# A two-layer decoder trunk on one core: the order of loads and weight splits in the wide phases of its MLP

## The chip, the cores and the metric

The kernel runs on one core of a Trainium2 chip. The metric is device time in microseconds of one execution; the number for the kernel before is the median of three runs. A profile of one execution, taken on the chip, gives spans, waits and transfers. In it PE is TensorE's matmuls, PEld its weight loads, DVE is VectorE, ACT is ScalarE, POOL is GpSimd and SP is SyncE. A "q" behind an engine's name (SPq) means its queue of issued transfers.

## The reference

The reference is a decoder trunk of two layers over 256 positions of width 2048, in float32. Each layer is a token mixer and then a gated MLP; each half is wrapped in RMS norms. The mixer of layer 0 is dilated window attention beside cross-attention to 256 memory tokens; that of layer 1 is stick-breaking attention beside the same cross-attention. The change touches the MLP, which is the same in both layers:

```python
def _conv_ffn(h, w_up, w_conv, b_conv, w_down):
    S = h.shape[1]
    u = h @ w_up
    gate, val = jnp.split(u, 2, axis=-1)
    gp = jnp.pad(gate, ((0, 0), (CONV_WIDTH - 1, 0), (0, 0)))
    acc = b_conv + gp[:, CONV_WIDTH - 1:CONV_WIDTH - 1 + S] * w_conv[CONV_WIDTH - 1]
    for j in range(CONV_WIDTH - 1):
        acc = acc + gp[:, j:j + S] * w_conv[j]
    return (jax.nn.silu(acc) * val) @ w_down
```

Here `h` is 256 x 2048, `w_up` is 2048 x 11264 (5632 gate columns, then 5632 value columns), the convolution runs over three positions, and `w_down` is 5632 x 2048.

## The kernel before, in words

**Precision.** Every product of two float32 matrices is made of three matmuls in a faster 32-bit format. Each operand is split into a high part (a rounding cast) and a low part (what the cast lost). `split` (L600) does it: ScalarE casts (L601), VectorE subtracts (L602). `mm3` (L127) then multiplies high by high, low by high and high by low.

**The MLP.** `ffn` (L724) walks over eleven groups of 512 columns of the gate and the value. Six groups are "narrow": they go tile by tile, 128 columns of one weight matrix against all positions. Five, those in `WIDE` (1, 3, 5, 7, 9), are "wide": `wide` (L613) makes the 512 gate and 512 value columns of a group for all 256 positions at once, with seven block products in place of eight, as in Strassen's scheme. It needs sums of weight blocks and sums of activation blocks. The activation sums are made once a layer by `sums_of_h` (L575); its last pieces are put behind the first wide phase's work by `rest` (L887). Behind each wide phase but the last, `downs` (L754) multiplies two finished groups by `w_down`.

**A wide phase** has eight units, u = 0 to 7, one for 256 rows of the weights. A unit holds:
- seven products of three matmuls each, `product` (L634), in seven PSUM banks: products 1, 2 and 3 with plain weights, products 7, 5, 6 and 4 with weight sums;
- one tile of the next narrow group beside them, `ws_beside` (L152). It is a Python generator in five steps: load the tile's weights of 1 MB (L156) and split the first half; split the second half; sixteen pairs of matmuls with the first half (L163); sixteen with the second half; the tile's sum out of PSUM, a copy on ScalarE (L175) and an addition on VectorE (L176). The eighth PSUM bank is the only one for it, so a tile's first matmul waits for the sum L176 of the tile before;
- the next unit's weights: `load` (L637) fetches 768 KB of raw weights (L640), `sums` (L643) makes two sums on VectorE (L646, L647), `plain` (L650) splits one and a half thousand columns of them, and `split_sums` (L659) splits the sums at the start of the next unit;
- for the unit after that, `first_sums` (L605): SyncE loads 512 KB (L608), and GpSimd adds another block to it with an accumulating transfer (L609) once the first has landed;
- two steps of elementwise work that earlier tiles left behind, run by `catch_up` (L91): the convolution, SiLU and the split of an activation pair.

**Buffers.** Raw weights of every kind share three buffers (`raw`); the high and low parts have four buffers each (`whi`, `wlo`); weight sums, activations and attention tensors share eleven (`sh`).

**Order.** A tile framework orders the instructions of each engine and places all waits. An instruction passed through `pin` (L96) is kept behind the one written before it on its engine, while `self.pinned` is set; it is set from the start of the unit loop (L673) to the end of the phase (L720). In the kernel before this holds matmuls, splits, sums and elementwise work of a phase, but not its loads: the framework may issue L156, L608 and L640 on SyncE in another order than the written one. The first load of raw weights (L663) and of the tile's weights (L669) stand ahead of L673. The written order of a unit's middle is:

```python
            if more:
                raw = load(u + 1)
                t = sums(ahead.pop(0), raw)
                after = beside[u + 1]()
                next(after)
            self.catch_up()
            next(b)
            next(b, None)
            if more:
                f = plain(raw)
                next(after)
```

In words: load the next unit's raw weights, sum them, load the next tile's weights and split their first half, do a leftover step, second half of this tile's matmuls, this tile's sum, then the plain splits, and the second half of the next tile's weights. On SyncE a unit writes the weight sum of u + 2 first (L685 or L687), then the raw weights of u + 1, then the tile's weights of u + 1.

Of the kernel before, what the change touches and what calls it, by code (L numbers as in the profile page):

```python
# [45 lines left out]
class Body:  # L46
# [49 lines left out]
    def pin(self, ins):  # L96
        return self.tc.keep_in_program_order(ins) if self.pinned else ins
# [54 lines left out]
    def ws_beside(self, out, src, h, done=None):  # L152


        raw = self.sb.tile([P, 2048], F32, name="raw", tag="raw", bufs=3)
        self.nc.sync.dma_start(raw, src)  # L156
        parts = []
        for i in range(2):
            parts.append([self.sb.tile([P, 1024], F32R, name=k, tag=k, bufs=4) for k in ("whi", "wlo")])
            self.split(*parts[i], raw[:, i * 1024:(i + 1) * 1024])  # L160
            yield
        b = self.bank("s")
        mm = lambda *o, **k: self.pin(self.nc.tensor.matmul(*o, **k))  # L163
        for half, (whi, wlo) in enumerate(parts):
            for k in range(8):
                kt = half * 8 + k
                ks = slice(k * P, (k + 1) * P)
                both, one = h[2][:, kt, :, :].rearrange("p a t -> p (a t)"), h[0][:, kt, :]
                if kt < KT - 1:
                    mm(b, whi[:, ks], both, start=kt == 0, stop=False)  # L170
                mm(b[:, 0:S], wlo[:, ks], one, start=False, stop=False)
                if kt == KT - 1:
                    mm(b, whi[:, ks], both, start=False, stop=True)
            yield
        self.pin(self.nc.scalar.copy(out, b[:, S:]))  # L175
        self.pin(self.nc.vector.tensor_add(out, b[:, 0:S], out))  # L176
        if done:
            done()
# [426 lines left out]
    def first_sums(self, src, u):  # L605

        d = self.sh([P, 1024])
        self.nc.sync.dma_start(d, src[u][:, 512:1536])  # L608
        self.nc.gpsimd.dma_start(d.rearrange("p (a n) -> p a n", a=2),  # L609
                                 src[u][:, 1536:].unsqueeze(1).to_broadcast([P, 2, 512]), accum_op=ALU.add)  # L610
        return d

    def wide(self, src, then, ahead, h, s, forms, r, beside):  # L613

        nc, n = self.nc, KT // 2
        ps = {i: self.bank("g" if i in (1, 2, 6, 7) else "s") for i in range(1, 8)}
        pin, add = self.pin, nc.vector.tensor_add
        half = lambda f, i: f[..., i * 512:(i + 1) * 512]

        def lhs(i, u):
            if i in (1, 2, 4):
                kt, t = 2 * u + (i != 1), int(i == 4)  # L630
                return [h[2][:, kt, a, t * P:(t + 1) * P] for a in range(2)]
            return [s[:, u, {5: 0, 6: 1, 7: 2, 3: 3}[i], a, :] for a in range(2)]

        def product(i, u, f, at):  # L634
            self.mm3(ps[i], *lhs(i, u), half(f[0], at), half(f[1], at), u == 0, u == n - 1)

        def load(u):  # L637

            raw = self.sb.tile([P, 2048], F32, name="raw", tag="raw", bufs=3)
            nc.sync.dma_start(raw[:, :1536], src[u][:, :1536])  # L640
            return raw

        def sums(d, raw):  # L643

            e = self.sh([P, 1024])
            pin(add(half(e, 1), half(d, 0), half(raw, 2)))  # L646
            pin(add(half(e, 0), half(e, 1), half(raw, 0)))  # L647
            return d, e

        def plain(raw):  # L650
            fa, fb = ([self.sb.tile([P, 1024], F32R, name=k, tag=k, bufs=4) for k in ("whi", "wlo")]
                      for _ in range(2))
            self.split(*fa, raw[:, 0:1024])
            self.split(*(half(f, 0) for f in fb), half(raw, 2))
            return fa, fb

        summed = [[forms[:, 2 * i + j, :] for j in range(2)] for i in range(2)]

        def split_sums(t):  # L659
            for of, parts in zip(t, summed):  # L660
                self.split(*parts, of)

        raw = load(0)  # L663

        high, low = self.splits[-4]
        with self.tc.issue_after(high.ins), self.tc.issue_after(low.ins):
            t = sums(ahead.pop(0), raw)
            split_sums(t)
        b = beside[0]()  # L669
# [3 lines that stand above are left out]
        self.pinned = True  # L673
        for u in range(n):
            more = u + 1 < n
            next(b)
            if u:
                split_sums(t)
            self.catch_up()
            fa, fb = f  # L680
            product(1, u, fa, 1)
            product(2, u, fa, 0)
            product(3, u, fb, 0)
            if u + 2 < n:
                ahead.append(self.first_sums(src, u + 2))  # L685
            elif then is not None:
                ahead.append(self.first_sums(then, u + 2 - n))  # L687
            if more:
                raw = load(u + 1)
                t = sums(ahead.pop(0), raw)  # L690
                after = beside[u + 1]()
                next(after)
            self.catch_up()
            next(b)
            next(b, None)
            if more:
                f = plain(raw)
                next(after)
            product(7, u, summed[0], 1)
            product(5, u, summed[0], 0)  # L700
            product(6, u, summed[1], 1)
            product(4, u, summed[1], 0)
            b = after
        a, g0, v0, v1 = (self.sc([P, 512]) for _ in range(4))
        more = lambda out, x, i: pin(add(out, ps[i], x))

        def scaled(out, i, t):
            pin(nc.vector.scalar_tensor_tensor(out, ps[i], r[:, t:t + 1], out, op0=ALU.mult, op1=ALU.add))

        pin(nc.scalar.copy(a, ps[1]))  # L710
        pin(nc.scalar.activation(g0, ps[1], AF.Copy, scale=r[:, 0:1]))  # L711
        scaled(g0, 2, 0)
        more(a, a, 6)
        more(v0, a, 5)
        more(v0, v0, 3)
        more(a, a, 7)
        more(v1, a, 5)
        pin(nc.scalar.activation(a, a, AF.Copy, scale=r[:, 1:2]))
        scaled(a, 4, 1)
        self.pinned = False  # L720
        self.catch_up(-1)
        return (g0, a), (v0, v1)
# [480 lines left out]
```

## Time and profile before

| what | value |
|---|---|
| three runs | 2288.51, 2296.90 and 2276.14 us; median 2288.51 |
| the profiled execution's own time | 2280.21 us |
| its span in the trace | 2278.4 us |
| TensorE matmuls busy | 2206.8 us (97%) |
| VectorE busy | 1651.4 us (72%) |
| ScalarE busy | 1283.7 us (56%) |
| TensorE clock granted, mean | 0.991 |
| transfers, mean rate | 227 GB/s |
| the ten wide phases, from first matmul to last product | 910.93 us |

The profile is of one execution. Matmuls overlap, so a busy TensorE is not TensorE at its peak. "Idle before <- X" gives the time an engine did nothing in front of an instruction, and what ended that; where an instruction waits for several things, the one that came last is named. The stretches view gives, for a window of time, the busy time of each engine, the number of its instructions, the granted clock and the share of time in which the sixteen DMA engines moved data. Line numbers in the profile are those of the kernel file.

### The profile page before, as it was taken

To read this page: it belongs to the slowest core of one execution; us is meant where nothing else is said; L and a number is where in the kernel's file an instruction comes from. 1 tells how busy PE (TensorE), PEld (TensorE's weight loads), DVE (VectorE), ACT (ScalarE), POOL (GpSimd) and SP (SyncE) were. 2 spreads that over 40 slices of the span, in tenths; PEclk is the share of its full clock that TensorE was granted. 3 is DMA by queue.
4 is the path that set the end of the run, shared out by engine and by line. 5 is a ranking of instruction groups with operands and counts; after the bars stand their busy time and mean duration, and the time that the engine had idled before them with its cause. 6 is when DMAs were issued, how large, how long until landed. Compare 5 with 4: busy or idle time off the path is not lost.

```text
span 2278.4 us, 28873 instructions
## 1 busy us (share of the span) xinstructions
PE 2206.8 (97%) x10962; PEld 1845.7 (81%) x10962; DVE 1651.4 (72%) x2175; ACT 1283.7 (56%) x1844; POOL 148.6 (7%) x168
## 2 busy tenths in 40 slices
PE   9999999989999999999999999999899999999998
PEld 7888888868878788787888888877688787887886
DVE  6567767977876867777774677579777768677786
ACT  7556556555555565555664555465565555656563
POOL 0000000010101111010000000000101011110100
PEclk9999999999999999999999999999999999999999
DMA  8745457676978979787745445576768789787974
GB/s 323 265 170 188 166 183 249 205 221 211 275 226 257 277 218 271 221 256 252 277 166 185 159 159 174 193 240 203 219 225 265 220 255 275 217 263 241 269 253 182
DMA packets 102381, 516.78 MB, mean 227 GB/s; under 512 B 10465, under 2 KB 10849, under 8 KB 61921
## 3 DMA queue, kind: packets, MB, share of 16 engines
q1 hardware_dynamic: 72288, 439.43, 54.5%
q0 software_dynamic: 29952, 75.51, 16.4%
q8 instruction: 86, 1.41, 0.2%
q14 instruction: 55, 0.44, 0.1%
HBM read 491.82 MB, written 23.07 MB: 226 GB/s over the span
## 4 chain that ended last, share of the span: by engine, by line
PE 78%; DMA 11%; DVE 5%; ACT 2%; issue 2%; SPq 0%; POOL 0%; POOLq 0%; ACTq 0%; DVEq 0%
PE ps_g L128 36%; PE ps_s L163 13%; PE ps_g L145 12%; PE ps_g L146 7%; DMA sh<-in_uw_dram 6%; PE ps_s L128 6%; DMA raw<-in_up_dram 4%; DVE wlo L602 3%; ACT whi L601 2%; PE ps_g L148 1%; PE ps_s L877 1%; DMA raw<-in_dn_dram 1%; PE ps_s L279 1%; DVE qk L176 0%; DMA raw<-in_wmv_dram 0%
## 5 line engine op out<-in xcount | busy, mean ns | idle before, releaser
L602 DVE TENSOR_TENSOR wlo<-raw,whi 128x1024 fp32r<-128x1024 f32 (+1 forms) x758 | 867.2, 1162 | 412.6 <-ACT whi L601 401.2
L601 ACT CAST whi<-raw 128x1024 fp32r<-128x1024 f32 (+1 forms) x758 | 743.8, 1003 | 665.8 <-DMA raw<-in_up_dram 273.2
L163 PE MATMUL ps_s<-h,whi 128*128 128x512 f32 x1280 | 477.0, 408 | 48.5 <-DVE qk L176 48.5
L128 PE MATMUL ps_g<-whi,sh 128*128 128x512 f32 x1488 | 466.1, 394 | 7.9 <-ACT sc L711 6.5
L145 PE MATMUL ps_g<-h,whi 128*128 128x512 f32 x1200 | 430.3, 401 | 0.8 <-DVE h L269 0.8
L163 PE MATMUL ps_s<-h,wlo 128*128 128x256 f32 x1280 | 352.7, 286 | 0.0
L146 PE MATMUL ps_g<-h,wlo 128*128 128x256 f32 x1280 | 345.8, 280 | 0.0
L163 PEld LDWEIGHTS ps_s<-h,whi 128*128 128x128 f32 x1280 | 247.1, 193 | 115.5 <-DVE qk L176 59.8
L128 PEld LDWEIGHTS ps_g<-whi,sh 128*128 128x128 f32 x1488 | 276.6, 188 | 71.4 <-ACT sc L711 10.9
L128 PE MATMUL ps_g<-wlo,sh 128*128 128x512 f32 x744 | 292.0, 393 | 0.0
L128 PE MATMUL ps_g<-whi,h 128*128 128x512 f32 x880 | 274.8, 393 | 0.5 <-ACT whi L601 0.5
L145 PEld LDWEIGHTS ps_g<-h,whi 128*128 128x128 f32 x1200 | 225.4, 188 | 52.1 <-DVE h L269 1.1
L163 PEld LDWEIGHTS ps_s<-h,wlo 128*128 128x128 f32 x1280 | 248.4, 194 | 9.6
L146 PEld LDWEIGHTS ps_g<-h,wlo 128*128 128x128 f32 x1280 | 241.6, 189 | 6.3
L602 DVE TENSOR_TENSOR x<-sh,x 128x1024 fp32r<-128x1024 f32 x160 | 189.1, 1217 | 0.0
L128 PEld LDWEIGHTS ps_g<-whi,h 128*128 128x128 f32 x880 | 160.0, 189 | 34.0 <-ACT whi L601 0.9
L128 PE MATMUL ps_g<-wlo,h 128*128 128x512 f32 x440 | 172.6, 393 | 1.1 <-DVE wlo L602 1.0
L601 ACT CAST x<-sh 128x1024 fp32r<-128x1024 f32 x160 | 161.4, 1049 | 9.0 <-DMA sh<-in_uw_dram 6.9
L128 PEld LDWEIGHTS ps_g<-wlo,sh 128*128 128x128 f32 x744 | 139.7, 188 | 31.8
L609 POOL DMA_DIRECT2D sh<-in_uw_dram x80 | 95.7, 1196 | 754.3 <-DMA sh<-in_uw_dram 497.3
L128 PE MATMUL ps_g<-x,h 128*128 128x512 f32 x480 | 137.6, 394 | 0.0
L128 PE MATMUL ps_s<-x,h 128*128 128x512 f32 x480 | 137.3, 394 | 0.0
(180 smaller groups left out, 2025.7 us busy)
## 6 DMA issues: line engine op xcount, KB each, us to landing
raw<-in_up_dram SPq DMA_DIRECT2D x96, 1024.0 KB, 5.4
raw<-in_dn_dram SPq DMA_DIRECT2D x88, 1024.0 KB, 6.4
raw<-in_uw_dram SPq DMA_DIRECT2D x80, 768.0 KB, 7.4
sh<-in_uw_dram SPq DMA_DIRECT2D x80, 512.0 KB, 9.0
sh<-in_uw_dram POOLq DMA_DIRECT2D x80, 512.0 KB, 10.0
raw<-in_wqk_a_dram SPq DMA_DIRECT2D x24, 1024.0 KB, 4.8
yout<-sh POOLq DMA_DIRECT2D x32, 512.0 KB, 8.3
raw<-in_wo_b_dram SPq DMA_DIRECT2D x16, 1024.0 KB, 4.9
```

Source lines behind the costliest of these rows:

```text
L128: mm = lambda *o, **k: self.pin(self.nc.tensor.matmul(*o, **k))
L145: mm(b, whi[:, ks], both, start=kt == 0, stop=False)
L146: mm(b[:, 0:S], wlo[:, ks], one, start=False, stop=False)
L148: mm(b, whi[:, ks], both, start=False, stop=True)
L163: mm = lambda *o, **k: self.pin(self.nc.tensor.matmul(*o, **k))
L279: self.nc.tensor.transpose(b[:, k * S + t * P:k * S + (t + 1) * P], self.x[:, t, kt * P:(kt + 1) * P], self.ident)
L601: high = self.pin(self.nc.scalar.copy(hi, of))
L602: low = self.pin(self.nc.vector.tensor_sub(lo, of, hi.bitcast(F32)))
L609: self.nc.gpsimd.dma_start(d.rearrange("p (a n) -> p a n", a=2), src[u][:, 1536:].unsqueeze(1).to_broadcast([P, 2, 512]), accum_op=ALU.add)
L877: nc.tensor.transpose(b[:, j * S + t * P:j * S + (t + 1) * P], of[t][:, f:f + P], self.ident)
```

## The change

It has two parts. The three kinds of loads in a wide phase are passed through `pin`, so that SyncE issues them in the written order: weight sum, raw weights, tile's weights. And in the middle of a unit the plain splits move from behind the tile's sum to ahead of it, while both halves of the next tile's load and split come behind it, where only the second half was.

```diff
@@ ws_beside @@
         raw = self.sb.tile([P, 2048], F32, name="raw", tag="raw", bufs=3)
-        self.nc.sync.dma_start(raw, src)
+        self.pin(self.nc.sync.dma_start(raw, src))
@@ first_sums @@
         d = self.sh([P, 1024])
-        self.nc.sync.dma_start(d, src[u][:, 512:1536])
+        self.pin(self.nc.sync.dma_start(d, src[u][:, 512:1536]))
@@ wide, load @@
-            nc.sync.dma_start(raw[:, :1536], src[u][:, :1536])
+            pin(nc.sync.dma_start(raw[:, :1536], src[u][:, :1536]))
@@ wide, the unit loop @@
             if more:
                 raw = load(u + 1)
-                t = sums(ahead.pop(0), raw)
                 after = beside[u + 1]()
-                next(after)
+                t, f = sums(ahead.pop(0), raw), plain(raw)
             self.catch_up()
             next(b)
             next(b, None)
             if more:
-                f = plain(raw)
+                next(after)
                 next(after)
```

GpSimd's accumulating transfer (L609) is not held to an order. The number of instructions, transfers and buffers is the same.

## The prediction

> **What bounds the kernel now.** I read the page first, then the stretches (busy time by window) over the wide phases, then the timeline engine by engine around the stalls, then the totals of waits. The page says that TensorE is the bound on average:
>
> ```profile
> span 2278.4 us, 28873 instructions
> PE 2206.8 (97%) x10962; PEld 1845.7 (81%) x10962; DVE 1651.4 (72%) x2175; ACT 1283.7 (56%) x1844; POOL 148.6 (7%) x168
> ...
> PE 78%; DMA 11%; DVE 5%; ACT 2%; issue 2%; SPq 0%; POOL 0%; POOLq 0%; ACTq 0%; DVEq 0%
> ```
>
> The 11% DMA in the chain that ended last says that transfers still end some of TensorE's waits. All that the change edits is in the ten wide phases (five in each layer, eight units each). I cut each phase at the first matmul of its unit 0, at that of unit 6, and behind unit 7's last product. Units 0 to 5, with the sum row over all ten phases last (columns: length; PE, PEld, DVE, ACT, POOL busy; TensorE clock, DMA share, GB/s):
>
> ```profile
> 421.69:494.43 72.74, 65.79 (x319) 53.90 (x318) 58.90 (x82) 36.74 (x50) 4.73 (x4) 0.98 0.74 229
> 570.34:633.34 63.00, 63.00 (x320) 52.98 (x319) 50.79 (x61) 35.65 (x47) 6.77 (x7) 1.00 0.90 280
> 707.48:770.98 63.50, 63.23 (x319) 52.97 (x318) 50.87 (x61) 35.64 (x47) 7.29 (x7) 1.00 0.95 285
> 1559.60:1633.13 73.53, 66.10 (x320) 53.77 (x318) 59.48 (x83) 36.87 (x50) 4.79 (x5) 0.98 0.75 229
> sum 657.02, PE 637.36 PEld 531.47 DVE 525.37 ACT 358.28 POOL 66.78; mean PE 63.74 PEld 53.15 DVE 52.54 ACT 35.83 POOL 6.68
> ```
>
> Units 6 and 7:
>
> ```profile
> 633.34:659.63 26.29, 22.80 (x107) 18.63 (x105) 17.55 (x21) 12.92 (x17) 3.31 (x3) 0.94 0.88 248
> 904.24:932.53 28.29, 23.67 (x107) 19.43 (x105) 19.15 (x23) 14.65 (x20) 3.58 (x3) 0.88 0.87 252
> 2178.36:2199.38 21.02, 21.02 (x107) 17.42 (x105) 17.78 (x22) 13.66 (x19) 0.15 (x1) 1.00 0.70 230
> sum 253.91, PE 224.04 PEld 183.90 DVE 183.44 ACT 140.32 POOL 27.73; mean PE 22.40 PEld 18.39 DVE 18.34 ACT 14.03 POOL 2.77
> ```
>
> The row 570.34:633.34 is six units in 63.00 us with TensorE busy for all 63.00: a unit without a stall takes 10.50 us. Two units take 21.02 in the last row. So the floor is 84 us a phase. Units 0 to 5 of all phases are 657.02 - 630.0 = **27.0 us** over it, of which the first phases of the two layers hold 9.7 + 10.5; units 6 and 7 are 253.91 - 210.0 = **43.9 us** over it. Together 70.9 us: that is all that the change can win. It is idle time and slower matmuls behind it (busy 224.04 against 210, clock 0.88).
>
> **Why units 6 and 7 stall.** The second phase of layer 0, in time (unit 6 begins at 633.34, as the row of units 6 and 7 has it, unit 5 10.5 us before that, unit 4 21):
>
> ```profile
> 613.26 0.33 SPq L156 DMA_DIRECT2D raw<-in_up_dram  x1
> 614.40 0.33 SPq L640 DMA_DIRECT2D raw<-in_uw_dram  x1
> 623.46 0.33 SPq L156 DMA_DIRECT2D raw<-in_up_dram  x1
> 624.60 0.33 SPq L640 DMA_DIRECT2D raw<-in_uw_dram  x1
> 624.98 0.91 SPq L608 DMA_DIRECT2D sh<-in_uw_dram  x2
> ...
> 633.10 2.44 POOL L609 DMA_DIRECT2D sh<-in_uw_dram  x2 [17.67 <-DMA sh<-in_uw_dram]
> ...
> 644.55 0.69 DVE L646 TENSOR_TENSOR sh<-sh,raw 128x512 f32<-128x512 f32 x1 [6.61 <-DMA sh<-in_uw_dram]
> ...
> 647.02 0.42 DVE L176 TENSOR_TENSOR qk<-ps_s,qk 128x256 f32<-128x256 f32 x1
> ...
> 647.49 0.51 PE L163 MATMUL ps_s<-h,whi 128*128 128x512 f32 x1 [3.49 <-DVE qk L176]
> ```
>
> SyncE issues no weight sum between 613 and 624.98, then two at once: unit 7's stands behind two loads that the code writes after it. It lands 8 us later, GpSimd's accumulating transfer (633.10) needs 11.4 more, VectorE waits 6.61 us for it, the tile's sum L176 stands behind that in VectorE's queue, and the next tile's matmul, which needs the same PSUM bank, waits 3.49 us.
>
> **Why the first phases stall in every unit.** Layer 1's first phase, units 2 to 3:
>
> ```profile
> 1585.86 0.33 SPq L156 DMA_DIRECT2D raw<-in_up_dram  x1
> 1598.37 0.33 SPq L156 DMA_DIRECT2D raw<-in_up_dram  x1
> ...
> 1593.24 1.05 ACT L601 CAST whi<-raw 128x1024 fp32r<-128x1024 f32 x1 [6.24 <-DMA raw<-in_up_dram]
> ...
> 1594.32 1.23 DVE L602 TENSOR_TENSOR wlo<-raw,whi 128x1024 fp32r<-128x1024 f32 x1 [3.15 <-ACT whi L601]
> 1595.57 0.42 DVE L176 TENSOR_TENSOR qk<-ps_s,qk 128x256 f32<-128x256 f32 x1
> 1596.52 2.96 DVE L602 TENSOR_TENSOR wlo<-raw,whi 128x1024 fp32r<-128x1024 f32 x3 [0.52 <-ACT whi L601]
> ```
>
> It is a loop. The up load goes out when the plain split frees a `raw` buffer (1585.86), lands 7.4 us later, is split first (ScalarE 1593.24, VectorE 1594.32), then comes the tile's sum (1595.57), then the plain splits (from 1596.52), and these free the buffer for the next up load (1598.37): 12.51 us round, two above the matmuls. Over the kernel:
>
> ```profile
> ACT whi L601 <- DMA raw<-in_up_dram: 273.2, 65, 7.2
> PE ps_s L163 <- DVE qk L176: 48.5, 24, 5.2
> ```
>
> **The change, part by part.** No instruction and no byte is added or taken away.
>
> *Order of loads.* Three loads of a unit are held to the written order on SyncE: weight sum of u+2, raw weights of u+1, up weights of u+1. Behind the up load at 613.26 would come unit 7's sum, not at 624.98: some 10 us earlier. With its own 8.1 + 11.4 us (624.98 to 633.10, 633.10 to 644.55) it would be there at about 634, and unit 6 asks for it at 637.9 (644.55 less the wait of 6.61). The stall of units 6 and 7 goes: -43.9 us. What is queued behind the sum is now the raw load and then the up load; both wait for it if no `sh` buffer is free. I count one `sh` tile for the memory keys (layer 0), four for the activations and four to five for sums at once, of eleven, so I put this wait at nothing; if the cover is missing, both loads and the up tile behind them are late by as much (third rival).
>
> *Plain splits ahead of the tile's sum.* The raw weights are loaded a unit ahead (the load at 614.40, in unit 4, is for the sums that unit 5 makes), so these splits wait for no fresh transfer, and they free `raw` some 3 us (one 1.23 split, L176's 0.42, and the gap in front) earlier. The up load goes out that much sooner and is asked for later, behind the tile's sum: it gets some 11 us to land (a unit of 10.5 us, and a cast's worth more), where it had the 7.4 of the loop. The loop of 12.51 us opens, and with it most of the 27.0 us.
>
> *The next tile's weights split behind the sum.* This is the price. The first split was done before the matmuls ended; now it stands between the tile's sum and the next tile's first matmul. A unit in which TensorE sets the pace has the pieces, since there the same engines do a split of the same size just behind the sum:
>
> ```profile
> 620.25 0.37 ACT L175 COPY qk<-ps_s 128x256 f32<-128x256 f32 x1 [0.33 <-PE ps_s L163]
> 620.52 2.52 ACT L601 CAST whi<-raw 128x1024 fp32r<-128x1024 f32 x3
> ...
> 621.61 2.96 DVE L602 TENSOR_TENSOR wlo<-raw,whi 128x1024 fp32r<-128x1024 f32 x3 [0.53 <-ACT whi L601]
> ...
> 622.84 0.39 PE L163 MATMUL ps_s<-h,whi 128*128 128x512 f32 x1
> ```
>
> Cast 620.52 + 1.05 = 621.57, subtraction 621.61 + 1.23 = 622.84, and the next tile begins at 622.84. It fits with nothing to spare: the low part is due at the second matmul (0.23 us on), its weights must be loaded before that, so I take 0.05 us a unit, 70 units: +3.5 us. From below the price is 0 (the row above); from above it is 0.7 us a unit (the rival of the split). I choose the low end because nothing stands between L175 and the cast in that row.
>
> *VectorE's time.* 50.79 / 6 = 8.5 us a unit of 10.5 (row 570.34), so it holds the pace. In the two first phases it does 58.90 - 50.79 = 8.1 us more (the sums of the activations, in units 0 and 1), 12.5 a unit there: some 5 us of delay stay in each, +10.
>
> *DMA.* In the row 707.48:770.98 the sixteen engines are busy 0.95 of the time at 285 GB/s. Moving a 512 KB sum and its accumulation into units 0 to 5 pushes that to about 1. From below this costs nothing, since 63.50 us were kept at that share; from above the rival below. I take 1.3 us in each of the seven phases in question (not the first ones and not the last, which loads no sums for a successor): +9.
>
> A phase of shorter units asks more of memory, so one more row bears on it, two stretches at the start of layer 0's fourth phase:
>
> ```profile
> 840.00:850.00 10.00, 10.00 (x53) 8.47 (x52) 6.12 (x8) 4.77 (x8) 2.05 (x2) 1.00 1.03 288
> 850.00:860.00 10.00, 10.00 (x53) 8.44 (x52) 6.41 (x7) 3.70 (x5) 1.20 (x1) 1.00 1.07 339
> ```
>
> The Trainium skill, Perfetto Trace Analysis, section Identifying the Most-Contended Engine, says to judge DMA by memory bandwidth used and not by the busy share of its sixteen engines. By that rule 285 of the 339 GB/s seen here leaves room, the +9 falls away and the time would be 2231; the row's share of 0.95 speaks the other way; which of them the kernel follows no row of before can show, and I keep +9.
>
> **Sum.** -70.9 + 3.5 + 10 + 9 = -48.4 us against the profiled execution: 2280.2 (span 2278.4 and 1.8 around it) becomes 2231.8. The runs shown have their median at 2288.5, 8.3 above that execution, so the forecast is **2240 us**, its own range 2222 to 2262.
>
> **Rivals.**
>
> *The DMA engines become the bound.* If the phases hold their pace only up to the 0.90 of the row 570.34:633.34, six units with the 60.3 us of transfers of the row 707.48:770.98 (0.95 of 63.50) need 67.0 us, 4.0 above 63; that is 5.3 for eight units and 37 for seven phases, where the sum has 9: about 2268. For it: the share. Against: that row itself, 63.50 us at 0.95.
>
> *The split behind the sum takes the place of the stall* (the other side). Place: VectorE's and ScalarE's queues between L175 and the next tile. Any lateness of the tile's sum is now followed by 1.05 + 1.23 us in series before TensorE may go on, with only the 2.6 us of four products (620.25 to 622.84) as cover. If the sum comes 1 us late in each of 70 units, because convolution steps, two weight sums and two plain splits all stand ahead of it, that is +70 - 48.4: about 2310. From 0.7 us a unit on it is slower than before. For it: zero slack in the row. Against: 8.5 of 10.5 us of VectorE's work.
>
> *The order does not bring the sums forward.* If the sum of unit 7 still waits for an `sh` buffer until unit 5, units 6 and 7 keep their 43.9 us, and the gain is 27.0 less 13.5: about 2275. For it: SyncE issued no sum in unit 4 (613.26 to 623.46), and a shortage of buffers would do that. Against: the count above.
>
> **How the numbers follow.** Forecast 0.62, DMA bound 0.13, order without effect 0.13, split in the way 0.12. Range 2222 to 2283: it leaves out the last rival and the tail under 2222 (all stalls gone and DMA free would be near 2220). About 1% (23 us, so 2266 and 2311) is what a measurement of this kernel can tell from no change. Faster: 0.62 and part of two rivals, 0.70; same 0.20; slower 0.10.
>
> **What would show it.** Right: a sum issued in every unit and ahead of the raw load; GpSimd's accumulations one per unit; units 6 and 7 near 21 us in the stretches with a clock of 1.00; the waits for up loads far under 273 us. Price right: waits of L163 of under 0.1 us, now ended by L602. Wrong: waits of 1 us ended by L602 in most units (split in the way), VectorE still waiting for `sh<-in_uw` in unit 6 (order), or DMA shares of 1.0 with units of 11 us and more.

## The result and the profile after

The changed kernel takes **2205.45 us** (median of four runs, 2204.71 to 2208.49) beside 2286.61 us for the kernel before in the same comparison (2276.14 to 2296.90). The ratio is 0.965, 95% interval 0.960 to 0.969: 3.5% faster. The forecast of 2240 us had the direction and the two stalls right, but the gain is 35 us larger, and the time lies under the range's low end of 2222.

The page of the changed kernel: its span, the busy times, and the engines' shares of the chain that ended last.

```profile
span 2203.1 us, 28992 instructions
...
PE 2184.6 (99%) x10962; PEld 1837.5 (83%) x10962; DVE 1651.4 (75%) x2175; ACT 1296.0 (59%) x1844; POOL 149.1 (7%) x168
...
PE 96%; DVE 2%; issue 1%; DMA 0%; SPq 0%; ACT 0%; POOL 0%; POOLq 0%; DVEq 0%; ACTq 0%
```

The page counts 119 instructions more than before, none of them among the counted work of the five engines. DMA's 11% of the chain are gone; TensorE's own work makes up 96% of it. The profiled execution took 2204.87 us, 75.3 less than the one of before. The ten wide phases, each now cut as a whole (length; PE, PEld, DVE, ACT, POOL busy; TensorE clock, DMA share, GB/s):

```profile
421.53:508.91 87.38, 85.05 (x425) 70.48 (x424) 78.86 (x107) 53.48 (x70) 8.31 (x7) 1.00 0.91 268
...
684.44:768.51 84.07, 84.07 (x425) 70.72 (x424) 70.64 (x85) 51.82 (x67) 9.25 (x8) 1.00 0.97 289
...
1518.54:1607.14 88.60, 86.34 (x425) 71.85 (x424) 79.04 (x107) 53.39 (x70) 8.34 (x7) 0.98 0.90 265
...
1782.67:1866.74 84.07, 84.07 (x425) 70.72 (x424) 70.54 (x85) 51.91 (x67) 9.23 (x8) 1.00 0.98 291
...
sum 848.55, PE 843.96 PEld 708.12 DVE 722.51 ACT 521.85 POOL 85.19; mean PE 84.40 PEld 70.81 DVE 72.25 ACT 52.18 POOL 8.52
```

The eight later phases sit on the floor of 84 us, with TensorE busy all the time. Only the layers' first phases are longer, by 3.4 and 4.6 us. The phases gave back 910.93 - 848.55 = 62.4 us. That leaves 12.9 us of the span's 75.3 which came from outside the phases. Most of that lies in the eight stretches between two phases of a layer (last row of the view for before, then for after):

```profile
sum 375.90, PE 369.43 PEld 302.46 DVE 258.92 ACT 226.99 POOL 19.09; mean PE 46.18 PEld 37.81 DVE 32.36 ACT 28.37 POOL 2.39
```

```profile
sum 365.83, PE 365.83 PEld 301.76 DVE 247.61 ACT 218.16 POOL 28.84; mean PE 45.73 PEld 37.72 DVE 30.95 ACT 27.27 POOL 3.60
```

That is 10.1 us, and the stretch behind the last phase gave 2.2 more (79.0 to 76.8). In the changed kernel TensorE is busy in every microsecond of these stretches. The prediction did not look at them.

The order of loads in the second phase of layer 0 (unit 4 begins at 596.7, unit 6 at 617.7), SyncE's queue:

```profile
594.83 0.64 SPq L608 DMA_DIRECT2D sh<-in_uw_dram  x1
597.81 0.33 SPq L640 DMA_DIRECT2D raw<-in_uw_dram  x1
603.76 0.33 SPq L156 DMA_DIRECT2D raw<-in_up_dram  x1
604.14 0.42 SPq L608 DMA_DIRECT2D sh<-in_uw_dram  x1
608.32 0.33 SPq L640 DMA_DIRECT2D raw<-in_uw_dram  x1
614.26 0.33 SPq L156 DMA_DIRECT2D raw<-in_up_dram  x1
```

For every unit a sum goes out, ahead of the raw load. Unit 7's goes out at 594.83, 22.9 us ahead of unit 6; in the kernel before it went out 8.4 us ahead of it. GpSimd's accumulations stand at 592.55, 603.24 and 614.49, one a unit. TensorE's waits in L163, where L176 ended 48.5 us of them, have become these two rows of the whole kernel:

```profile
PE ps_s L163 <- DVE qk L176: 2.4, 2, 1.2
...
PE ps_s L163 <- DVE wlo L602: 1.1, 2, 0.6
```

All four waits stand in the layers' first phases.

### The profile page after: what moved, and what is told of

Read it like the earlier page. It is cut to its first block, busy times and chain, and to the rows that moved or that the text cites. A ratio compares the mean times of both kernels' runs of the same rounds, so it can differ in the third digit from the quotient of the medians.

```text
span 2203.1 us, 28992 instructions
## 1 busy us (share of the span) xinstructions
PE 2184.6 (99%) x10962; PEld 1837.5 (83%) x10962; DVE 1651.4 (75%) x2175; ACT 1296.0 (59%) x1844; POOL 149.1 (7%) x168
## 4 chain that ended last, share of the span: by engine, by line
PE 96%; DVE 2%; issue 1%; DMA 0%; SPq 0%; ACT 0%; POOL 0%; POOLq 0%; DVEq 0%; ACTq 0%
PE ps_g L128 42%; PE ps_s L163 20%; PE ps_g L145 13%; PE ps_s L128 10%; PE ps_g L146 7%; PE ps_g L148 1%; PE ps_s L876 1%; DVE wlo L602 1%; PE ps_s L279 1%; DMA raw<-in_wmv_dram 0%; PE ps_s L330 0%; PE ps_s L357 0%; PE ps_s L436 0%; PE ps_s L393 0%; PE ps_s L454 0%
## 5 line engine op out<-in xcount | busy, mean ns | idle before, releaser
L602 DVE TENSOR_TENSOR wlo<-raw,whi 128x1024 fp32r<-128x1024 f32 (+1 forms) x758 | 867.0, 1163 | 337.1 <-ACT whi L601 328.5
L601 ACT CAST whi<-raw 128x1024 fp32r<-128x1024 f32 (+1 forms) x758 | 751.4, 1004 | 437.5 <-PE ps_g L128 207.3
L163 PE MATMUL ps_s<-h,whi 128*128 128x512 f32 x1280 | 462.6, 398 | 2.4 <-DVE qk L176 2.4
L163 PE MATMUL ps_s<-h,wlo 128*128 128x256 f32 x1280 | 347.1, 281 | 1.2 <-DVE wlo L602 1.1
L163 PEld LDWEIGHTS ps_s<-h,whi 128*128 128x128 f32 x1280 | 241.2, 188 | 55.2 <-ACT x L601 3.2
L163 PEld LDWEIGHTS ps_s<-h,wlo 128*128 128x128 f32 x1280 | 242.3, 189 | 16.0 <-DVE wlo L602 2.3
L602 DVE TENSOR_TENSOR x<-sh,x 128x1024 fp32r<-128x1024 f32 x160 | 189.2, 1219 | 0.0
L609 POOL DMA_DIRECT2D sh<-in_uw_dram x80 | 97.8, 1226 | 673.4 <-DMA sh<-in_uw_dram 347.7
L175 ACT COPY qk<-ps_s 128x256 f32<-128x256 f32 x80 | 29.9, 374 | 186.1 <-PE ps_s L163 186.1
## 6 DMA issues: line engine op xcount, KB each, us to landing
sh<-in_uw_dram POOLq DMA_DIRECT2D x80, 512.0 KB, 10.6
```

What stands on the lines that cost most here:

```text
L601: high = self.pin(self.nc.scalar.copy(hi, of))
L602: low = self.pin(self.nc.vector.tensor_sub(lo, of, hi.bitcast(F32)))
```

## Experiments

The time of the kernel before moves between comparisons (2284 to 2287 us); the tables give each run's median and its ratio to the runs of before beside it. Two runs repeat the sum of weights, one adds a cast whose result nothing reads, and one loads columns that nothing reads.

### Each part alone

The changed kernel without the three pins, so with the moved splits alone:

```diff
-        self.pin(self.nc.sync.dma_start(raw, src))
+        self.nc.sync.dma_start(raw, src)
...
-        self.pin(self.nc.sync.dma_start(d, src[u][:, 512:1536]))
+        self.nc.sync.dma_start(d, src[u][:, 512:1536])
...
-            pin(nc.sync.dma_start(raw[:, :1536], src[u][:, :1536]))
+            nc.sync.dma_start(raw[:, :1536], src[u][:, :1536])
```

> The moved splits alone; the three loads are free again. Theory (two separate faults): the loop of up load, first split, tile's sum and plain splits opens, so units 0 to 5 lose most of their 27 us, but unit 7's weight sum still goes out late and units 6 and 7 keep their 43.9 us: between 2255 and 2275 us, with VectorE still waiting for sh<-in_uw in unit 6. Rival (one fault, the loop): the freed buffer lets everything go out sooner and the time is within 10 us of the changed kernel, 2205 to 2215.

And the kernel before with the three pins, so with the order alone (the same three lines the other way round):

> The written order of the loads alone; the splits stand as before. Theory (two separate faults): units 6 and 7 fall to about 21 us a phase and the waits behind the last product go, together 44 to 55 us, while the first phases keep units of about 12 us and the second units their 0.5 to 1.5 us: 2225 to 2240 us. Rival (one fault, the order): 2205 to 2215 us. Second rival: the held order puts an up load behind a waiting weight sum and, still split ahead of the tile's sum, it stalls more units than before: over 2285 us.

| kernel | us | ratio (95%) | in the phases | outside | ScalarE's wait for up loads | VectorE's wait for sums |
|---|---|---|---|---|---|---|
| before | 2286.61 | 1 | 910.9 | 1367.5 | 273.2 | 64.2 |
| moved splits alone | 2248.43 | 0.985 (0.980 to 0.990) | 887.7 | 1355.7 | 3.1 | 60.3 |
| pins alone | 2282.83 | 1.000 (0.998 to 1.003) | 893.3 | 1387.5 | 312.8 | none |
| both | 2205.45 | 0.965 (0.960 to 0.969) | 848.6 | 1354.6 | 3.3 | none |

Both expectations missed. The moved splits alone came out 7 us under 2255: the first phases fall from 101.3 and 101.0 us to 88.6 and 88.5, as the theory had it, but the late sums do not stay in units 6 and 7: in the later phases they lengthen units 6 and 7, units 1 and 2, or both. The pins alone did what the second rival said, at 2 us under its price.

The two waits come apart cleanly. The row of the sums for the moved splits alone, then the rows of up loads and of the phase's end for the pins alone:

```profile
DVE sh L646 <- DMA sh<-in_uw_dram: 60.3, 17, 6.0
```

```profile
ACT whi L601 <- DMA raw<-in_up_dram: 312.8, 64, 6.9
...
PE ps_g L128 <- ACT sc L711: 21.7, 10, 4.0
```

The order cures the late sums, and the moved split cures the late up loads. But the gains do not add: the pins alone are worth nothing (17.6 us less in the phases, 20.0 more outside), and on top of the moved splits they are worth 43 us. With the pins alone a sum follows right behind the up load on SyncE's queue:

```profile
620.49 0.33 SPq L156 DMA_DIRECT2D raw<-in_up_dram  x1
620.87 1.72 SPq L608 DMA_DIRECT2D sh<-in_uw_dram  x1
```

and the up load's landing grows. The transfer rows for before and for the pins alone (count, KB, us to landing):

```profile
raw<-in_up_dram SPq DMA_DIRECT2D x96, 1024.0 KB, 5.4
```

```profile
raw<-in_up_dram SPq DMA_DIRECT2D x96, 1024.0 KB, 6.6
```

While the next up load waits for the split of this one, 1.2 us more of landing is up to 1.2 us more on each round of the loop that the prediction described: the stalls of units 6 and 7 spread over units 1 to 6, most of which now take 10.6 to 12.7 us. The kernel with both has a landing of 6.1 us and pays nothing for it, since nothing waits for it any more. What lengthens the landing (the sum behind it on the queue) is read from the order of issue, and wasn't tried apart.

### The missed 12.9 us

The same two runs answer where they came from. The moved splits alone have the eight stretches between phases at 45.72 to 45.74 us; the pins alone have 396.72 us in them, 20.8 more than before. So it is the split's place. Before, TensorE idled for 6.5 of the 375.90 us, and most of that is this wait, here over all ten phase ends:

```profile
PE ps_g L128 <- ACT sc L711: 6.5, 10, 1.6
```

The pins alone have 21.7 us of it, the changed kernel none. How it works, at the end of the second phase of layer 0 in the kernel before, ScalarE and then TensorE:

```profile
657.52 2.00 ACT L601 CAST whi<-raw 128x1024 fp32r<-128x1024 f32 x2 [3.16 <-DMA raw<-in_dn_dram]
...
660.69 0.69 ACT L711 ACTIVATE sc<-ps_g,small 128x512 f32<-128x512 f32 x1
...
661.44 0.74 PE L128 MATMUL ps_g<-whi,sh 128*128 128x512 f32 x2 [1.64 <-ACT sc L711]
```

TensorE needs a PSUM bank that L711 empties. L711 stands behind the casts of the second `w_down` tile in ScalarE's queue, and these wait 3.16 us for that tile's load (the first tile's casts ran at 652.03 and 653.31 without such a wait). The load is late because it needs one of the three `raw` buffers, and the last unit's plain splits, in VectorE's queue from 647.35 on, hold one. SyncE, before and then after:

```profile
635.10 0.33 SPq L107 DMA_DIRECT2D raw<-in_dn_dram  x1
...
649.20 7.42 SPq L107 DMA_DIRECT2D raw<-in_dn_dram  x3
```

```profile
618.84 0.33 SPq L107 DMA_DIRECT2D raw<-in_dn_dram  x1
...
624.78 17.12 SPq L107 DMA_DIRECT2D raw<-in_dn_dram  x4
```

The second `w_down` load goes out at 649.20, 10.4 us ahead of the phase's end (659.63), and lands 8.2 us later. In the changed kernel it goes out at 624.78, 13.9 us ahead of the end (638.71), lands at 632.55, and its cast runs at 633.36 without a wait for it. That the split's place causes this is shown by the two runs; the way through the buffer and ScalarE's queue is read from the timeline and wasn't tried apart.

### The suspected costs, one by one

**DMA.** The raw load takes all 1024 KB of its block in place of 768:

```diff
-            pin(nc.sync.dma_start(raw[:, :1536], src[u][:, :1536]))
+            pin(nc.sync.dma_start(raw, src[u]))
```

> The changed kernel with 256 KB more in every raw load (the last quarter is loaded and not used). If the busy share of the DMA engines is the bound (it is 0.97 to 0.98 in the busiest phases, and the addition is about 0.07 of a unit), six or more phases get 3 to 5 us longer: 2225 to 2245 us. If the rate of memory is what counts (291 GB/s become about 316, and 339 were seen), units stay at 10.52 us and the time within 5 us of 2205.

Measured 2205.19 us, ratio 0.966 (0.963 to 0.969): nothing.

```profile
814.48:898.53 84.05, 84.05 (x425) 70.71 (x424) 70.60 (x85) 51.81 (x67) 9.26 (x8) 1.00 1.00 308
```

The sixteen engines are busy for the whole of the phase, at 308 GB/s, and its length is 84.05. A share of 1.00 is no bound here; the loads only land later (7.1 us for an up load, 6.1 without the extra bytes) and are ahead of their use by more than that.

**The split behind the tile's sum.** First a cast of 512 columns is put between the tile's sum and the first split; then the first half of the split is moved ahead of the sum, but left behind the plain splits:

```diff
+                x = self.sb.tile([P, 512], BF16, name="junk", tag="junk", bufs=1)
+                pin(nc.scalar.copy(x, raw[:, 512:1024]))
                 next(after)
                 next(after)
```

> The changed kernel with one more ScalarE cast of 512 columns, result unused, between the tile's sum and the next tile's first split (about 0.53 us of ScalarE's queue). If that stretch has no slack, as the prediction says, each of 70 units gets 0.5 us longer: about 2240 us. If there is slack of half a microsecond or more, the time stays within 5 us of 2205.

```diff
                 t, f = sums(ahead.pop(0), raw), plain(raw)
+                next(after)
             self.catch_up()
...
-                next(after)
                 next(after)
```

> The changed kernel with the first half of the next tile's weights split ahead of the tile's sum again, but behind the plain splits. Theory (the loop opens because the plain splits free their buffer before the tile's sum is waited for; where the first half stands does not matter as long as it comes behind them): within 4 us of 2205, and the units without a stall back at 10.50. Rival (the up load must be asked for behind the tile's sum, or its landing holds that sum up): 2225 us or more, with ScalarE waiting for raw<-in_up in most units.

The cast: 2234.08 us, ratio 0.978 (0.975 to 0.982), 28.6 us more than the changed kernel. The split ahead: 2205.64 us, ratio 0.967 (0.963 to 0.971), the same. A later phase and TensorE's waits with the cast, then the same phase with the split ahead:

```profile
690.13:777.17 87.04, 85.86 (x425) 70.17 (x424) 70.33 (x85) 55.23 (x74) 9.25 (x8) 1.00 0.94 282
```

```profile
PE ps_s L163 <- DVE wlo L602: 12.6, 70, 0.6
```

```profile
686.17:770.12 83.95, 83.95 (x425) 70.74 (x424) 71.74 (x85) 53.05 (x67) 9.25 (x8) 1.00 0.99 291
```

With the cast all 70 units that have a successor wait, and in each phase seven units grow by 0.43 us (10.52 to 10.95): nearly the whole of the cast's 0.49 (ScalarE's 55.23 us less 51.82, for seven casts). So the prediction's "it fits with nothing to spare" is right to 0.1 us. And the split's place behind the sum costs 84.07 - 83.95 = 0.12 us a phase. What mattered in the move was that the plain splits come ahead of the sum, not where the first half of the next tile's split stands. The run with the split ahead differs from the pins alone in the place of the plain splits only; up loads land in 6.6 us in both, and it takes 77 us less.

**Sums first.** The sum for u + 2 is written behind the raw load and the tile's load, and held there:

```diff
-            if u + 2 < n:
-                ahead.append(self.first_sums(src, u + 2))
-            elif then is not None:
-                ahead.append(self.first_sums(then, u + 2 - n))
...
                 after = beside[u + 1]()
                 t, f = sums(ahead.pop(0), raw), plain(raw)
+            if u + 2 < n:
+                ahead.append(self.first_sums(src, u + 2))
+            elif then is not None:
+                ahead.append(self.first_sums(then, u + 2 - n))
```

> The changed kernel with the weight sum's load written behind the raw load and the tile's load instead of ahead of them; all three are still held to the written order. Theory (what counts is that no sum is skipped and that each goes out early; one place later in SyncE's queue is one up load's wait, some 10 us, and landing takes 8.6 + 10.6 of the 28 us that there are): a few units stall, 2208 to 2235 us. Rival (holding the order is all that counts): within 3 us of 2205. Second rival (the sum must be ahead of the raw load): 2240 us or more, units 6 and 7 as long as before.

Measured 2243.35 us, ratio 0.984 (0.980 to 0.988): the time of the second rival, and the expectation missed. The place is not the rival's, though. In most phases the long units (11 to 13 us) lie among units 1 to 4, and in two phases only among the later ones too. The sums are late again, and it costs 37 us in the phases:

```profile
sum 885.90, PE 854.42 PEld 709.13 DVE 721.68 ACT 522.12 POOL 96.98; mean PE 85.44 PEld 70.91 DVE 72.17 ACT 52.21 POOL 9.70
```

```profile
DVE sh L646 <- DMA sh<-in_uw_dram: 61.0, 22, 5.4
```

A fixed order alone isn't the gain. It is this order. The reason is argued, not tried: the sum is the load with two transfers in series (8.1 us to land, then 10.6 for the accumulation, by the transfer rows of the changed kernel), so it has the longest way to its use.

**Buffers of the sums.** Ten `sh` buffers in place of eleven:

```diff
-        return self.sb.tile(shape, dtype, name="sh", tag="sh", bufs=11)
+        return self.sb.tile(shape, dtype, name="sh", tag="sh", bufs=10)
```

> The changed kernel with ten buffers for the weight sums in place of eleven. Theory: in the changed kernel the buffers of the sums are not the limit, because the loads come in the written order and the sums land well ahead of their use; within 5 us of 2205. Rival: with one buffer less a sum's load waits for the tile's sum two tiles before to let go, that holds the raw load behind it on SyncE's queue, and the phase slips by some tenths of a us a unit: 2220 us or more.

Measured 2228.27 us, ratio 0.975 (0.971 to 0.979): the rival's size, 22.8 us, but not in its place. The steady units keep 10.5 us. The loss is in units 0 and 1 of layer 0's third to fifth phases (8 to 9 us each), and 3.4 us lie ahead of layer 0's first phase. ScalarE, SyncE (its wait, then its issues) and TensorE at the first of the three, which begins at 688.07:

```profile
670.82 1.07 ACT L764 COPY sh<-ps_g 128x512 f32<-128x512 f32 x2 [4.64 <-DMA yout<-sh]
```

```profile
SPq L608 <- DVE sh L646: 10.0, 1, 10.0
```

```profile
687.38 0.33 SPq L608 DMA_DIRECT2D sh<-in_uw_dram  x1
687.80 0.71 SPq L640 DMA_DIRECT2D raw<-in_uw_dram  x1
688.60 0.43 SPq L156 DMA_DIRECT2D raw<-in_up_dram  x1
```

```profile
703.12 0.80 PE L163 MATMUL ps_s<-h,whi 128*128 128x512 f32 x1 [4.43 <-ACT whi L601]
```

Between phases the tiles of `downs` take `sh` buffers too. With ten, ScalarE's copy into such a tile waits for the write of an earlier one to land, once in each stretch between layer 0's phases (16.3 us in all; none with eleven), and what stands behind it in ScalarE's queue is late. Then the sum's load stands at the head of SyncE's queue for 10.0 us, until VectorE's first weight sum of the phase is done (L646, at 687.36). It goes out 0.7 us ahead of the phase, where with eleven it went out 10.8 us ahead (673.64 for a phase that begins at 684.44). The raw and up loads written behind it follow at once: the raw load is 0.3 us ahead of the phase, and was 8.7 us ahead (675.75). This is the block that the prediction named under the order of loads. Its count of nine or ten tiles leaves out those of `downs`; with them eleven are just enough. That it hits layer 0 alone agrees with the one tile of memory keys in that count, but wasn't tried apart.

### VectorE and the first phases

Four more additions of the second weight sum in each unit, and then two:

```diff
-            pin(add(half(e, 0), half(e, 1), half(raw, 0)))
+            for _ in range(5):
+                pin(add(half(e, 0), half(e, 1), half(raw, 0)))
```

> The changed kernel with the second of the two weight sums made five times instead of once, ahead of the tile's sum: four more VectorE additions of 0.61 to 0.69 us in each of 70 units (the result is the same). This is the price of a late tile's sum, the rival of the prediction that was to make the kernel slower. Theory: VectorE does 8.8 us a unit, 1.7 less than the 10.5 of the matmuls, so 2.5 us more make a unit about 0.8 to 1.0 us longer: 2260 to 2275 us. Rival (each late sum costs its lateness and the split behind it, and slows the matmuls too): over 2290 us. If VectorE's slack hides it: under 2215 us.

> The changed kernel with the weight sum's second addition made three times over (the same result each time): two more VectorE instructions of some 0.68 us a unit, 1.36 us, where the run with four of them cost 85 us. VectorE has 70.6 us of work in a later phase of 84.07 us, so 8.83 us a unit; with 1.36 more it comes to 10.2, just under the 10.51 of TensorE. Theory: what counts is VectorE's throughput, the later phases stay at 84 to 85 us, and only the first phases, where the activation sums bring VectorE to 78.9 us already, become longer, by 5 to 6 us each on top of what they have; 2210 to 2225 us. Rival: what counts is how late the splits come behind the additions in the queue, whatever VectorE's share; then every unit pays about half of what four of them cost, 0.4 to 0.5 us, 32 to 40 us in all, and the time is 2240 us or more.

Four cost 85.0 us (2290.47 us, ratio 1.003, 1.001 to 1.005); two cost 11.3 (2216.79 us, ratio 0.970, 0.964 to 0.976). The later phase at 706 us with four, then a first and a later phase with two:

```profile
706.25:797.32 91.07, 86.45 (x425) 70.15 (x424) 89.59 (x115) 51.93 (x67) 9.25 (x8) 1.00 0.91 269
```

```profile
421.95:513.86 91.91, 86.69 (x425) 71.67 (x424) 89.16 (x122) 54.42 (x71) 8.31 (x7) 0.98 0.84 256
...
689.82:774.34 84.52, 84.16 (x425) 70.58 (x424) 79.78 (x99) 52.20 (x67) 9.25 (x8) 1.00 0.98 289
```

VectorE may be busy for 79.78 of 84.52 us, 94%, at a price of half a microsecond; at 98% it sets the pace. The expectation for two held, though the first phases grew by 4.5 and 3.2 us instead of 5 to 6. That for four, 2260 to 2275, fell short: the first phases went to 101.4 us, and each later phase has a unit of 12.67 beside steady ones of 11.45. The time is the rival's, but not by slower matmuls: the clock of the row is 1.00. So the first phases' 8 us should be VectorE's, and their activation sums should be the thing to move. First the last three sums of each layer are all made on the last step of the narrow group before; then two are made a step from the third on; then the latter with the first half of the split ahead, as above:

```diff
-        for i in range(5):
-            self.later(i + 2, lambda i=i: make(i)())
+        for i in range(8):
+            self.later(min(i + 2, 7), lambda i=i: make(i)())
...
-        self.behind_this(*(lambda i=i: rest(i) for i in range(5, KT // 2 + 1)))
```

> The changed kernel with all eight sums of activations made in the narrow group ahead of the first wide phase; the last three were made behind its first two units. Theory (VectorE overloaded by these sums in units 0 and 1 is what is left in the first phases, 3.4 and 4.6 us): the two phases lose most of their excess, 2198 to 2202 us. Rival (that excess is the start of a phase, with its own splits and loads late): within 1.5 us of 2205. A second rival is that the narrow group's tiles now wait for VectorE: slower by 2 us or more.

```diff
-            self.later(min(i + 2, 7), lambda i=i: make(i)())
+            self.later(2 + i // 2, lambda i=i: make(i)())
```

> The changed kernel with the activation sums of the next layer spread two to a step from the third step on, so that all eight are made inside the narrow group and none is left for the first wide phase. Theory: the two first phases, 87.38 and 88.60 us in the changed kernel beside 84.07 in the others, lose most of the 8.0 us, because it is VectorE work in their units 0 to 3 that makes them longer; about 2197 to 2203 us. Rival: the sums are only moved to VectorE's queue in the narrow group, where the run that put three of them on the last step paid 20 us for unit 0; then not under 2204 us. The run with them on the last step gave 2216, and this one has to lie under it if piling up was its cause.

> The run above with the first half of the next tile's split put ahead of the tile's sum but behind the plain splits. Theory: the place of that half decides nothing here either (2205.64 beside 2205.45 without the spreading), so it stays within 2 us of the run above. Rival: with VectorE's extra work gone from the first phases the 0.07 us a unit that is left of the split behind the sum comes back, 70 units, some 5 us less than the run above.

| kernel | us | ratio (95%) | first phases | the others |
|---|---|---|---|---|
| changed kernel | 2205.45 | 0.965 (0.960 to 0.969) | 87.4, 88.6 | 84.07 |
| three sums on the last step | 2216.06 | 0.971 (0.968 to 0.974) | 93.4, 92.5 | 83.8 |
| two a step | 2207.79 | 0.967 (0.964 to 0.970) | 84.1, 84.1 | 84.06 |
| two a step, split ahead | 2207.80 | 0.967 (0.964 to 0.969) | 84.0, 84.0 | 83.95 |

The cause is confirmed and the cure fails: both expectations of a gain missed (2198 to 2202, 2197 to 2203), and in each a rival had the time. With three sums on the last step, unit 0 of the first phases takes 20.1 and 19.1 us, and TensorE waits 14.4 us there for VectorE. With two a step the first phases are like the others, all units at 10.5; yet the total is no better, since the 20 us ahead of the phase became longer. The place of the split's first half decides nothing here either, as expected. With two a step, the first phase, the 20 us ahead of it, and the matmul that waited there:

```profile
428.14:512.21 84.07, 84.07 (x425) 70.72 (x424) 71.09 (x87) 51.65 (x67) 8.31 (x7) 1.00 0.93 282
```

```profile
407.82:428.14 20.32, 16.58 (x86) 14.08 (x85) 20.28 (x39) 12.55 (x19) 1.21 (x1) 0.92 0.40 129
```

```profile
418.60 0.39 PE L146 MATMUL ps_g<-h,wlo 128*128 128x256 f32 x1 [3.74 <-DVE wlo L602]
```

and the 20 us ahead of it in the changed kernel:

```profile
401.21:421.53 20.32, 20.32 (x117) 17.66 (x116) 20.32 (x41) 14.88 (x22) 1.21 (x1) 1.00 0.55 170
```

VectorE was already full there, 20.32 of 20.32 us. The work was moved from one place where VectorE has no room to another: the phases gained 8.0 us, and the two layers' starts lost 6.6 and 5.7.

## Why the prediction missed

Its steps against the profiled executions; it made 2231.8 us of 2280.2, the chip 2204.87. The miss of 26.9 us has four terms:

- **"Together 70.9 us: that is all that the change can win": failed, 12.9 us.** The floor of 84 us a phase was right, and so was the reading of the two loops. But the bound was drawn around the lines that the change edits. What those lines let go of, the `raw` buffer, is used next by the `w_down` loads at the phase's end, and these held ScalarE's queue and through it a PSUM bank. The prediction asked what is late when a stall goes. It did not ask what else comes early when a buffer does.
- **DMA, +9: failed, 9 us.** The later phases hold 84.07 us at shares up to 0.98, and a third more bytes on the raw load (1024 KB in place of 768) change nothing. The Trainium skill, Perfetto Trace Analysis, section Identifying the Most-Contended Engine, wants DMA judged by the memory bandwidth used instead of the engines' busy share; these runs agree with it (84.05 us at a share of 1.00 and 308 GB/s). The prediction worked out the time by that rule, 2231, and kept the row.
- **The split behind the tile's sum, +3.5: right in kind, 0.6 measured** (eight phases 0.07 us over 84; against the run with the split ahead, 0.12 a phase). The low end was the right one, and the slack is as thin as it said.
- **The first phases, +10: right, 8.0 measured** (3.4 and 4.6), with the cause it gave. The 1.2 us between the two go with a slower clock behind the same waits (last section).

To these comes the step from the profiled execution to the median: 8.3 us were added, as the runs of before stood, and 0.6 were due. The kernel before scatters over 21 us, the changed one over 4. That the landings scattered, for which TensorE no longer waits, is argued from the waits. Two runs of ten executions each fit it: the pins alone, where up loads are waited for, scatter over 21.8 us, and the run with four more additions, just as slow, but through VectorE, over 1.7. 26.9 + 8.3 - 0.6 makes the 34.6 us between forecast and result.

What held: units 6 and 7 at 21 us and a clock of 1.00; a sum in every unit ahead of the raw load; ScalarE's waits for up loads at 3.3 us from 273. The sign of the price, short waits of L163 ended by L602, did not show: the later phases have no wait in L163 at all, and of the 3.5 us in the first phases L176 ends 2.4. Of the rivals, DMA as the bound is ruled out by the longer load. The split in the way is 0.1 us away from mattering, but is covered in every unit. The missing buffers are one buffer away, as the run with ten shows. The 27.0 and 43.9 us were not two separate gains, though, as the prediction and the expectations had them: as the runs of each part alone show, fixing the order without opening the loop of the up load gives nothing in total.

## What to carry to other kernels

When a move frees a shared buffer earlier, list every load that takes that buffer next, also behind the end of the stage that is edited; the waits there belong to the gain. A wait can only be priced while the loop that it lies on is known: a reorder that lengthens one landing by a microsecond costs nothing if the load is ahead of its use, and up to a microsecond a round if it is not. And before work is moved off an engine that is too busy, read that engine's share in the place where it is going.

## What the hardware showed beyond that

A wait of TensorE cost more than its length. With the activation sums two a step, TensorE idled by 3.74 us until 418.60, and from 419.55 on ran at half its clock for a while (two pairs of matmuls from before the wait, two from behind it, and the row of the slow stretch):

```profile
412.10 0.40 PE L145 MATMUL ps_g<-h,whi 128*128 128x512 f32 x1
...
412.46 0.40 PE L145 MATMUL ps_g<-h,whi 128*128 128x512 f32 x1
...
420.13 0.63 PE L145 MATMUL ps_g<-h,whi 128*128 128x512 f32 x1
...
420.77 0.63 PE L145 MATMUL ps_g<-h,whi 128*128 128x512 f32 x1
```

```profile
419.55:422.96 3.41, 3.41 (x14) 2.93 (x13) 3.41 (x6) 0.66 (x2) 0.00 (x0) 0.50 0.99 336
```

A pair takes 0.36 us before the wait and 0.64 in the slow stretch, at a granted clock of 0.50. Over 3.41 us that loses some 1.5 us more (an estimate from these pairs), and the granted clock of the 20 us is 0.92. In layer 1 a wait of 3.8 us made the start of the phase 5.7 us later. The Trainium skill, TensorE: Matmul & The Clock Gate, Part 1, says that a window of some 3.4 us without work halves the clock, and that about as long under work brings it back; this trace agrees, with 3.74 us of wait and 3.41 us of half clock.

But the clock also fell behind shorter waits. In the changed kernel the first phases of both layers have the same three waits of TensorE, 0.5, 1.2 and 0.6 us, and then differ in unit 1, here of layer 0 and of layer 1:

```profile
434.10:445.48 11.38, 10.80 (x53) 8.92 (x54) 11.28 (x17) 5.72 (x9) 1.19 (x1) 1.00 0.88 237
```

```profile
1531.11:1544.06 12.95, 12.37 (x53) 10.21 (x54) 11.87 (x18) 5.61 (x9) 1.19 (x1) 0.87 0.84 242
```

No wait there is longer than 1.2 us, and yet in layer 1 the clock is 0.87 and the unit 1.6 us longer. What decides between the two is not shown.
